# The last two token tiles of mLSTM's v and o share one pass over the weights

## The chip, the core and the metric

The kernel runs on one core of a Trainium2 chip. The time is device microseconds from the start to the end of one execution, lower is better. Three executions of the kernel before are given, and one more was recorded by the profiler; the trace of that one is what is read here.

## The reference, cut to what matters

One sequence of 512 tokens with 1024 features passes through two layers. The change touches one stage of the first layer, the mLSTM mixer: two of its four projections, `v` and `o`.

```python
def mlstm_mixer(h, w_in, i_bias, f_bias, conv_w, conv_b, norm_w, w_out):
    proj = h @ w_in
    qk = jax.nn.silu(causal_conv(proj[..., :2 * M_QK], conv_w, conv_b))
    q = split_heads(qk[..., :M_QK], M_HEADS)
    k = split_heads(qk[..., M_QK:], M_HEADS) * (M_DQK ** -0.5)
    v = split_heads(proj[..., 2 * M_QK:2 * M_QK + M_V], M_HEADS)
    o = proj[..., 2 * M_QK + M_V:2 * M_QK + 2 * M_V]
    ...
    hh = mlstm_chunkwise(q, k, v, i_pre, f_pre)
    hh = merge_heads(head_rmsnorm(hh, norm_w)) * jax.nn.sigmoid(o)
    return hh @ w_out
```

Every sub-layer is also modulated by (shift, scale, gate) = silu(c) @ ada_w + ada_b. That product is done on VectorE, in 80 small portions that are strewn through the stages (`ar`).

## The kernel before, in words

**Weights.** All dense weights lie in one list in the order in which they are used. A slot is 128x1024 values. Two slots come with one DMA into a tile `raw` (2 buffers, issued by SyncE). ScalarE copies a slot into a rounded tile `whi`, VectorE makes the rest `wlo` = raw - whi; both have 5 buffers (L400). A product is three matmuls: hi*hi, hi*lo, lo*hi. `Weights.get` (L234) returns a piece of a slot; it lets a slot go when its last user has passed and issues the ScalarE copies of slots for which a buffer is free (`want`). The VectorE subtractions of these are kept in a list and issued (`low`, L205) when `get` first reaches a new slot; with a subtraction the next load of `raw` is issued.

**The stage.** `main()` in `mlstm` computes the last two tiles of q and k, then v in two halves of 512 columns (a = 0, 1), then o in two halves. A half has four slots and four token tiles (`v00` to `v03`, `v10` to `v13`, `o00` and so on: half, tile). `tile_tok` computes one token tile: 24 matmuls over the four slots of the half. The first three tiles leave the slots where they are; the fourth lets each go when it has passed over it. So the slots of the next half find buffers only in the fourth tile, except the first of them, which has the fifth buffer. In this stage the slots 9 to 12 are v's first half, 13 to 16 the second, 17 to 20 and 21 to 24 those of o; `wlo14` is the second slot of v's second half, `wlo22` that of o's second half.

**After a tile.** A tile of v is copied to SBUF by ScalarE (`va`), then `ada()` issues one portion of the modulation on VectorE (`ar`, 128x1024, read from DRAM into 2 buffers; the load into a buffer is issued behind the portion that read it). A tile of o is copied by VectorE (`og`), then `ada(2)` issues two portions. After the four tiles of a half of o ScalarE applies the sigmoid.

**What sets the order around it.** `weave` (L336) runs `main()` and, at each `yield` of it, steps of side work as long as a plan of the engines' times says that VectorE and ScalarE are less than 3 us behind TensorE; two side jobs are open at a time. The side jobs are the gates, the convolutions (`conv`: ScalarE writes `qk`, VectorE adds three taps to it from the accumulator, later a silu; f = 0 to 7, `qk0` to `qk7`), the four head pairs (`pair`: scores `S`, decay `dt`, transposed keys `kp` and `kt`, states `cu` and `st`, outputs `nu`), and `close` (products `y`, transposes `tph`). All accumulators, those of side work too, come from one pool of 8 PSUM banks (L396); a tile takes a bank that an earlier one has left, and its first matmul waits until that one has been read. What `weave` and `Weights` decide is fixed when the program is built; on the chip each engine runs its own list in order.

After o, `out_proj` computes `m_out`; its first heads are closed by `y` on VectorE and `tph` on TensorE.

Of the kernel before, what the change touches and what calls it, by code (L numbers as in the profile page):

```python
# [10 lines left out]
F32 = mybir.dt.float32  # L11
# [4 lines left out]
AF = mybir.ActivationFunctionType  # L16
# [5 lines left out]
P = 128  # L22
D = 1024
T = 512
KT = D // P
NC = T // P
# [18 lines left out]
def _plan():  # L45
    plan, at = [], {}

    def add(name, blocks):
        at[name] = len(plan)
        plan.extend(blocks)  # L50

    k8 = range(KT)
    add("m_g0", [("m_qk", k, f) for k in k8 for f in (8, 0, 4, 1, 5, 2, 6)])
    add("m_qk", [("m_qk", k, f) for f in (3, 7) for k in k8])
    add("m_v", [("m_v", k, 4 * a + j) for a in range(2) for k in k8 for j in range(4)])
    add("m_o", [("m_o", k, 4 * a + j) for a in range(2) for k in k8 for j in range(4)])
    out_order = [(k, f) for k in k8 for f in range(4)] + [(k, f) for k in range(4) for f in range(4, 8)] + \
        [(k, f) for f in range(4, 8) for k in range(4, 8)]
    add("m_out", [("m_w_out", k, f) for k, f in out_order])
    for s in range(2):  # L60
        f0 = s * ET
        b = [("ffn", k, f) for k in k8 for f in (f0, FT + f0, f0 + 1, FT + f0 + 1)] if s == 0 else []
        for f in range(f0 + (2 if s == 0 else 0), f0 + ET):
            b += [("ffn", k, x) for x in (f, FT + f) for k in k8]
        add(f"f_in{s}", b)
        add(f"f_down{s}", [("ffn_w_down", f0 + f, d) for d in k8 for f in range(ET)])
    add("h_first", [("h_w_in", k, f) for k in k8 for f in (0, 8, 1, 9)])
    for what in H_ORDER:
        if what[0] == "h":
            h = int(what[1])  # L70
            add(what, [("h_w_in", k, f) for f in (h, 8 + h, h + 1, 9 + h) for k in k8])
        elif what[0] == "g":
            add("h_" + what, [("h_w_in", k, 24 + int(what[1]) + f) for f in range(4) for k in k8])
        else:
            add("h_" + what, [("h_w_in", k, 16 + 4 * int(what[1]) + j) for k in k8 for j in range(4)])
    add("h_out", [("h_w_out", k, f) for k, f in out_order])
    at["moe"] = len(plan)
    return plan, at


PLAN, AT = _plan()
# [306 lines left out]
class Kernel:  # L388
# [264 lines left out]
            if k % 2:  # L653
                yield

    def tile_tok(self, b, i, acc):

        mm = self.nc.tensor.matmul
        ts = slice(i * P, (i + 1) * P)
        for k in range(KT):  # L660
            hi, lo = self.W.get(b + 4 * k, 4, i == NC - 1)
            xh, xl = self.hn[k][0][:, ts], self.hn[k][1][:, ts]
            mm(acc, xh, hi, start=k == 0, stop=False)
            mm(acc, xh, lo, start=False, stop=False)
            mm(acc, xl, hi, start=False, stop=k == KT - 1)
            if k % 2:
                yield

    def out_proj(self, name, hh, l, side=lambda: None):

# [47 lines left out]
    def mlstm(self):  # L718
        nc, tc = self.nc, self.tc
        V, S = nc.vector, nc.scalar  # L720
        ident = self.C("ident")
        with ExitStack() as ctx:
# [5 lines left out]
            with tc.tile_pool(name="adf", bufs=6) as adf, tc.tile_pool(name="rawf", bufs=2) as rawf:  # L728
# [6 lines left out]
                accs = self.group_first("m_g0", 7, self.norm(0, 0, (a0,)))  # L735
            self.dump("hn0", [x for h in self.hn for x in h])
            self.big = ctx.enter_context(tc.tile_pool(name="big0", bufs=24))
            va_p = ctx.enter_context(tc.tile_pool(name="va", bufs=8))
# [28 lines left out]
            va, ys, og, hh, rsd, rows = {}, {}, {}, {}, {}, []  # L767
# [47 lines left out]
            def main():  # L815
                for n, f in enumerate((3, 7)):
                    acc = self.ps(f"qk{f}")
                    yield from self.tile_ws(AT["m_qk"] + 8 * n, self.hn, acc)
                    todo.append((f, acc))
                    self.ada()  # L820
                for a in range(2):
                    for i in range(NC):
                        acc = self.ps(f"v{a}{i}")
                        yield from self.tile_tok(AT["m_v"] + 32 * a, i, acc)
                        t = va_p.tile([P, 4, P + 1], F32, name=f"va{a}{i}", tag="va")
                        S.activation(t[:, :, 0:P], acc.rearrange("p (h d) -> p h d", h=4), AF.Copy)
                        nc.gpsimd.memset(t[:, :, P:P + 1], 1.0)
                        va[a, i] = t
                        self.ada()
                for a in range(2):  # L830
                    for i in range(NC):
                        acc = self.ps(f"o{a}{i}")
                        yield from self.tile_tok(AT["m_o"] + 32 * a, i, acc)
                        t = og[a, i] = self.slot(f"og{a}{i}")
                        V.tensor_copy(t, acc)
                        self.ada(2)
                    for i in range(NC):
                        S.activation(og[a, i], og[a, i], AF.Sigmoid)

# [110 lines left out]
            sides += [(lambda h=h: (h // 4, NC - 1) in og and h in rsd, close(h)) for h in range(4)]  # L950
            self.W.ahead = 4
            weave(nc.plan, main(), sides, 2, 0.0, 3.0)
            self.W.ahead = 3
            self.dump("y", [ys[a, c] for a in range(2) for c in range(NC)])
# [61 lines left out]
    def hgrn(self):  # L1016
        nc, tc = self.nc, self.tc
        V, S = nc.vector, nc.scalar
        ident = self.C("ident")
        with ExitStack() as ctx:  # L1020
# [19 lines left out]
            QK, LF, Q1, v, g, hh = {}, {}, {}, {}, {}, {}  # L1040
# [32 lines left out]
            def proj():  # L1073
                accs = self.group_first("h_first", 4, self.norm(1, 0))
                self.dump("hn1", [x for h in self.hn for x in h])
                for k in range(KT):
                    nc.gpsimd.dma_start(self.X[k], self.x[k])
                z = self.nrm.tile([P, T], F32, name="zero", tag="tmp")
                nc.gpsimd.memset(z, 0.0)
                for j in range(2):  # L1080
                    for i in range(0, NSLOT, P):
                        n = min(P, NSLOT - i)
                        nc.gpsimd.dma_start(self.XG[j][i:i + n], z[:n])
                evac(0, (accs[:2], accs[2:]))
                self.router()
                yield
                for what in H_ORDER:
                    w, n = what[0], int(what[1])
                    ps = []
                    for i in range(4):  # L1090
                        acc = self.ps(f"h{what}{i}")
                        if w == "h":
                            yield from self.tile_ws(AT[what] + 8 * i, self.hn, acc)
                            ps.append(acc)
                            if i == 3:
                                while not done >= {n - 3, n - 4}:
                                    yield "wait"
                                evac(n, (ps[:2], ps[2:]))
                            continue
                        t = new(f"{what}{i}", "vg", 12)  # L1100
                        if w == "v":
                            yield from self.tile_tok(AT["h_" + what], i, acc)
                            S.activation(t, acc, AF.Copy)
                            v[n, i] = t
                        else:
                            yield from self.tile_ws(AT["h_" + what] + 8 * i, self.hn, acc)
                            S.activation(t, acc, AF.Copy)
                            g[n + i] = t
                            if i >= 2:
                                gated(range(n + (i - 2) * 3, n + i + 1))  # L1110

            def gated(hs):

                for h in hs:
                    S.activation(g[h], g[h], AF.Silu)
                for h in hs:
                    if h in hh:
                        V.tensor_mul(hh[h], hh[h], g[h])
                    on.add(h)
# [146 lines left out]
            def main():  # L1266
                yield from proj()
                for _ in range(H - 2):
                    while next(out) == "wait":
                        yield "wait"  # L1270
                    yield
# [591 lines left out]
```

## Time and profile before

| | us |
|---|---|
| three executions | 1566.93, 1577.71, 1581.69 (median 1577.71) |
| the profiled execution | 1568.58 |
| its span, first to last instruction | 1566.8 |
| TensorE busy in it | 1490.4 (95%) |
| VectorE busy | 1087.0 (69%) |
| ScalarE busy | 845.4 (54%) |
| mean granted TensorE clock | 0.978 |

The stage of this change lies between about 76 and 216 us of the span. A row of the profile's waits says which engine waited for which, for how long in total, how often, and the longest. A row of the timeline gives start and duration (us), engine, line, operation, out<-in, shape, count, and in brackets the idle time of the engine before it and what ended it. Nearly all lines read L317, a helper through which every instruction is recorded, so rows are told apart by their tiles. The duration of a matmul is longer than its distance to the next, since matmuls are pipelined: 0.39 us stands for a distance of 0.23 us at the full clock, 0.63 for one of 0.43 at half of it.

### The profile page before, as it was taken

What the parts mean: (1) busy time and instruction counts of PE and PEld (TensorE: products, weight loads), DVE (VectorE), ACT (ScalarE), POOL (GpSimd) and SP (SyncE); (2) the same over time, 40 slices, a digit from 0 to 9 for tenths busy, and PEclk for the clock granted to TensorE, in tenths of its full rate; (3) what the DMA queues carried; (4) which work ended last, traced back from release to release, by engine and by line L of the source; (5) the groups of instructions that cost most, each with busy time, mean ns of one, the idle gap of its engine ahead of it and who ended that gap; (6) DMA issues with size and microseconds to landing.
All of it is one profiled execution on the core that took longest, in us unless ns stands there. A gap on an engine that the chain in (4) does not pass through costs nothing. (4 is left out here: it accounts for less than half of the span.)

```text
span 1566.8 us, 23572 instructions
## 1 busy us (share of the span) xinstructions
PE 1490.4 (95%) x8935; PEld 1310.8 (84%) x8935; DVE 1087.0 (69%) x1978; ACT 845.4 (54%) x1562; POOL 135.0 (9%) x213
## 2 busy tenths in 40 slices
PE   4989999999999999999999998999999999999995
PEld 3867776888888888688888875999999999999993
DVE  6886774655455545695977654687877878788795
ACT  5466333432222322365647543687786868777663
POOL 0041000000000000300000010501010010100142
PEclk9999999999999999999999999999999999999996
DMA  9462641445445553532102132788787887878782
GB/s 377 159 208 79 212 161 56 161 187 212 154 171 205 182 190 110 208 136 98 55 28 81 54 105 108 273 290 303 250 283 266 282 274 253 299 263 268 278 302 90
DMA packets 80854, 300.47 MB, mean 192 GB/s; under 512 B 8036, under 2 KB 8084, under 8 KB 79712
## 3 DMA queue, kind: packets, MB, share of 16 engines
q1 hardware_dynamic: 69424, 266.36, 47.9%
q0 software_dynamic: 11312, 32.56, 6.3%
q8 instruction: 72, 1.18, 0.3%
q14 instruction: 46, 0.38, 0.1%
HBM read 280.78 MB, written 18.09 MB: 191 GB/s over the span
## 5 line engine op out<-in xcount | busy, mean ns | idle before, releaser
L317 DVE TENSOR_TENSOR wlo<-raw,whi 128x1024 fp32r<-128x1024 f32 x403 | 489.6, 1222 | 106.4 <-ACT whi L317 104.3
L317 ACT ACTIVATE whi<-raw 128x1024 fp32r<-128x1024 f32 x403 | 422.0, 1055 | 182.0 <-DMA raw<-in_w 31.9
L317 PE MATMUL gu<-x,whi 128*128 128x304 f32 x1408 | 360.1, 345 | 2.1 <-DVE x L317 2.1
L317 PE MATMUL gu<-x,wlo 128*128 128x152 f32 x1408 | 328.5, 233 | 0.0
L317 PEld LDWEIGHTS gu<-x,wlo 128*128 128x128 f32 x1408 | 270.1, 192 | 0.0
L317 PEld LDWEIGHTS gu<-x,whi 128*128 128x128 f32 x1408 | 265.4, 189 | 2.5 <-DVE x L317 2.3
L317 PE MATMUL yd<-h,whi 128*128 128x304 f32 x704 | 181.6, 346 | 1.3 <-DVE h L317 1.3
L317 PE MATMUL yd<-h,wlo 128*128 128x152 f32 x704 | 163.8, 233 | 0.0
L317 PEld LDWEIGHTS yd<-h,wlo 128*128 128x128 f32 x704 | 134.5, 191 | 0.0
L317 PEld LDWEIGHTS yd<-h,whi 128*128 128x128 f32 x704 | 132.2, 188 | 1.6 <-DVE h L317 1.5
L317 DVE SCALAR_TENSOR_TENSOR ar<-ar,cond 128x1024 f32<-128x1024 f32 x80 | 98.4, 1232 | 3.9 <-DMA ar<-in_ada 3.8
L317 ACT ACTIVATE fhi<-fg 128x512 fp32r<-128x512 f32 x22 | 13.9, 633 | 114.3 <-DVE fg L317 114.3
L317 DVE TENSOR_TENSOR fg<-fg,fup 128x512 f32<-128x512 f32 x20 | 13.8, 688 | 82.7 <-PE fup L317 82.7
L317 PE MATMUL fd<-fhi,whi 128*128 128x512 f32 x176 | 69.6, 396 | 0.0
L317 PE MATMUL fd<-flo,whi 128*128 128x512 f32 x176 | 69.6, 396 | 0.0
L317 PE MATMUL fd<-fhi,wlo 128*128 128x512 f32 x176 | 69.6, 396 | 0.0
L317 ACT ACTIVATE t<-gu 128x152 f32<-128x152 f32 x176 | 47.9, 289 | 35.5 <-PE gu L317 33.5
L317 PE MATMUL fgp<-lo,whi 128*128 128x512 f32 x160 | 62.3, 389 | 0.0
L317 PE MATMUL fgp<-hi,whi 128*128 128x512 f32 x160 | 62.2, 389 | 0.0
L317 PE MATMUL fgp<-hi,wlo 128*128 128x512 f32 x160 | 62.2, 389 | 0.0
L317 PE MATMUL fup<-hi,whi 128*128 128x512 f32 x160 | 62.2, 389 | 0.0
L317 PE MATMUL fup<-lo,whi 128*128 128x512 f32 x160 | 62.2, 389 | 0.0
(404 smaller groups left out, 2988.5 us busy)
## 6 DMA issues: line engine op xcount, KB each, us to landing
raw<-in_moe SPq DMA_DIRECT2D x128, 1024.0 KB, 6.0
raw<-in_w SPq DMA_DIRECT2D x69, 1024.0 KB, 5.4
ar<-in_ada SPq DMA_DIRECT2D x80, 512.0 KB, 4.0
ad<-in_ada SPq DMA_DIRECT2D x8, 1024.0 KB, 14.8
XG<-zero POOLq DMA_DIRECT2D x18, 256.0 KB
xr<-XG POOLq DMA_DIRECT2D x28, 152.0 KB
raw<-in_moe SPq DMA_DIRECT2D x8, 512.0 KB, 3.5
Y<-yt POOLq DMA_DIRECT2D x14, 256.0 KB
```

The costliest lines, as they stand in the source:

```text
L317: r = f(*args, **kw)
```

## The change

`tile_tok` takes a list of tiles. The tiles 2 and 3 of every half of v and o go through the slots together: for each of the eight k, three matmuls for tile 2 and three for tile 3. Each slot is let go when both have passed over it, so the four go over 48 matmuls and not over 24. The copies of the two tiles and their portions of the modulation are issued after the shared pass, one tile behind the other. The shared pass yields to side work after every three matmuls, not six, and each copied tile is followed by one more yield. The second layer's use of `tile_tok` stays as it was (one tile in the list).

```diff
-    def tile_tok(self, b, i, acc):
+    def tile_tok(self, b, tiles, accs):
 
         mm = self.nc.tensor.matmul
-        ts = slice(i * P, (i + 1) * P)
         for k in range(KT):
-            hi, lo = self.W.get(b + 4 * k, 4, i == NC - 1)
-            xh, xl = self.hn[k][0][:, ts], self.hn[k][1][:, ts]
-            mm(acc, xh, hi, start=k == 0, stop=False)
-            mm(acc, xh, lo, start=False, stop=False)
-            mm(acc, xl, hi, start=False, stop=k == KT - 1)
-            if k % 2:
-                yield
+            hi, lo = self.W.get(b + 4 * k, 4, tiles[-1] == NC - 1)
+            for i, acc in zip(tiles, accs):
+                ts = slice(i * P, (i + 1) * P)
+                xh, xl = self.hn[k][0][:, ts], self.hn[k][1][:, ts]
+                mm(acc, xh, hi, start=k == 0, stop=False)
+                mm(acc, xh, lo, start=False, stop=False)
+                mm(acc, xl, hi, start=False, stop=k == KT - 1)
+                if k % 2 or len(tiles) > 1:
+                    yield
...
                 for a in range(2):
-                    for i in range(NC):
-                        acc = self.ps(f"v{a}{i}")
-                        yield from self.tile_tok(AT["m_v"] + 32 * a, i, acc)
-                        t = va_p.tile([P, 4, P + 1], F32, name=f"va{a}{i}", tag="va")
-                        S.activation(t[:, :, 0:P], acc.rearrange("p (h d) -> p h d", h=4), AF.Copy)
-                        nc.gpsimd.memset(t[:, :, P:P + 1], 1.0)
-                        va[a, i] = t
-                        self.ada()
+                    for tiles in ((0,), (1,), (2, 3)):
+                        accs = [self.ps(f"v{a}{i}") for i in tiles]
+                        yield from self.tile_tok(AT["m_v"] + 32 * a, tiles, accs)
+                        for i, acc in zip(tiles, accs):
+                            t = va_p.tile([P, 4, P + 1], F32, name=f"va{a}{i}", tag="va")
+                            S.activation(t[:, :, 0:P], acc.rearrange("p (h d) -> p h d", h=4), AF.Copy)
+                            nc.gpsimd.memset(t[:, :, P:P + 1], 1.0)
+                            va[a, i] = t
+                            self.ada()
+                            yield
                 for a in range(2):
...
+                        for i, acc in zip(tiles, accs):
+                            t = og[a, i] = self.slot(f"og{a}{i}")
+                            V.tensor_copy(t, acc)
+                            self.ada(2)
+                            yield
```

The program has as many TensorE instructions as before, 8467 rows of its list, and no VectorE or ScalarE instruction is added. The order changes at these places.

TensorE in v's first half, at the first scores `S0`, `S1` of head pair 0. Before, they stand near the end of tile v02, when v03 has no accumulator yet:

```order
L317 MATMUL v02_723<-whi11_520,lo4_364 128x512
L317 MATMUL v02_723<-whi11_520,hi5_393 128x512
L317 MATMUL v02_723<-wlo11_521,hi5_393 128x512
L317 MATMUL v02_723<-whi11_520,lo5_399 128x512
L317 MATMUL S0_748<-qk0_526,qk4_531 128x128
L317 MATMUL S1_749<-qk0_526,qk4_531 128x128
```

Now:

```order
L317 MATMUL v03_724<-whi9_457,lo1_256 128x512
L317 MATMUL v02_723<-whi10_516,hi2_286 128x512
L317 MATMUL v02_723<-wlo10_517,hi2_286 128x512
L317 MATMUL v02_723<-whi10_516,lo2_292 128x512
L317 MATMUL S0_749<-qk0_526,qk4_531 128x128
L317 MATMUL S1_750<-qk0_526,qk4_531 128x128
```

Both accumulators, v02 and v03, are open when the scores come, and 33 matmuls of the two tiles stand behind the scores, where 30 stood. The bank that v03 took from the convolution of `qk2` before (`m_g05`) is now the bank of `S1`.

VectorE at the turn from v's first half to its second, from the copy `dec0` of pair 0 to the first `wlo` that is needed. Before:

```order
L317 COPY dec0_806<-wb0_674 128x4
L317 TENSOR_TENSOR qk0_526<-qk0_526,wb0_674 128x512
L317 SCALAR_TENSOR_TENSOR qk3_818<-qk3_537,vec_93,qk3_818 128x511
L317 SCALAR_TENSOR_TENSOR qk3_818<-qk3_537,vec_93,qk3_818 128x510
L317 SCALAR_TENSOR_TENSOR qk3_818<-qk3_537,vec_93,qk3_818 128x509
L317 SCALAR_TENSOR_TENSOR ar4_721,mod0_119<-ar4_721,cond_91 128x1024
L317 TENSOR_TENSOR wlo14_787<-raw7_524,whi14_786 128x1024
```

Now:

```order
L317 COPY dec0_805<-wb0_667 128x4
L317 TENSOR_TENSOR qk0_526<-qk0_526,wb0_667 128x512
L317 SCALAR_TENSOR_TENSOR qk7_817<-qk7_570,vec_93,qk7_817 128x511
L317 SCALAR_TENSOR_TENSOR qk7_817<-qk7_570,vec_93,qk7_817 128x510
L317 SCALAR_TENSOR_TENSOR qk7_817<-qk7_570,vec_93,qk7_817 128x509
L317 SCALAR_TENSOR_TENSOR ar3_661,mod0_119<-ar3_661,cond_91 128x1024
L317 SCALAR_TENSOR_TENSOR ar4_721,mod0_119<-ar4_721,cond_91 128x1024
L317 TENSOR_TENSOR wlo14_743<-raw7_524,whi14_742 128x1024
```

The three taps of `qk3` now stand ahead of `dec0`; those of `qk7`, which stood behind the four `wlo`, have come ahead of them, and the portion `ar3`, which stood ahead of pair 0's two `dt`, now comes right ahead of `ar4`.

VectorE at the turn from o's first half to its second, from the copy of tile o03 (before) or o02 (now) to the first `wlo` that is needed. Before:

```order
L317 COPY og03_1545<-o03_1511 128x512
L317 SCALAR_TENSOR_TENSOR ar15_1506,mod0_119<-ar15_1506,cond_91 128x1024
L317 TENSOR_TENSOR mod0_119<-mod0_119,vec_93 128x8
L317 SCALAR_TENSOR_TENSOR ar16_1509,mod0_119<-ar16_1509,cond_91 128x1024
L317 TENSOR_TENSOR wlo22_1519<-raw11_1254,whi22_1518 128x1024
```

Now:

```order
L317 COPY og02_1537<-o02_1478 128x512
L317 SCALAR_TENSOR_TENSOR ar13_1473,mod0_119<-ar13_1473,cond_91 128x1024
L317 SCALAR_TENSOR_TENSOR ar14_1476,mod0_119<-ar14_1476,cond_91 128x1024
L317 COPY og03_1545<-o03_1479 128x512
L317 SCALAR_TENSOR_TENSOR ar15_1540,mod0_119<-ar15_1540,cond_91 128x1024
L317 TENSOR_TENSOR mod0_119<-mod0_119,vec_93 128x8
L317 SCALAR_TENSOR_TENSOR ar16_1543,mod0_119<-ar16_1543,cond_91 128x1024
L317 TENSOR_TENSOR wlo22_1493<-raw11_1376,whi22_1492 128x1024
```

`og02` and its two portions were done a tile earlier; now they stand behind the shared pass too, ahead of `og03`. At the end of o's second half the same eight rows stand ahead of the products `y` (`og12`, `ar21`, `ar22`, `og13`, `ar23`, two small sums, `ar24`, sixteen `y`).

## Rows read from the trace of the kernel before

**Rows 1.** Busy time, share of the span, instructions: part 1 of the page.

```profile
PE 1490.4 (95%) x8935; PEld 1310.8 (84%) x8935; DVE 1087.0 (69%) x1978; ACT 845.4 (54%) x1562; POOL 135.0 (9%) x213
```

**Rows 2.** Waits of TensorE, 60 to 300 us: total us, times, longest.

```profile
PE v L317 <- DVE wlo L317: 5.1, 1, 5.1
PE o L317 <- DVE wlo L317: 3.9, 1, 3.9
PE f_in L317 <- ACT hi L317: 3.0, 1, 3.0
PE nu L317 <- DVE dt L317: 2.4, 1, 2.4
PE tph L317 <- DVE y L317: 2.1, 2, 1.7
```

**Rows 3.** Timeline of TensorE at the turn to v's second half.

```profile
109.61 0.79 PE L317 MATMUL v<-wlo,hi 128*128 128x512 f32 x1 [5.14 <-DVE wlo L317]
```

**Rows 4.** Timeline of VectorE ahead of the same turn.

```profile
94.72 2.32 DVE L317 SCALAR_TENSOR_TENSOR qk<-m_g,vec,qk 128x511 f32<-128x511 f32 x3 [3.35 <-ACT qk L317]
...
102.18 1.57 DVE L317 COPY dec<-wb 128x4 f32<-128x4 f32 x1
103.41 0.68 DVE L317 TENSOR_TENSOR qk<-qk,wb 128x512 f32<-128x512 f32 x1
104.97 2.31 DVE L317 SCALAR_TENSOR_TENSOR qk<-qk,vec,qk 128x511 f32<-128x511 f32 x3 [0.88 <-ACT qk L317]
107.20 1.21 DVE L317 SCALAR_TENSOR_TENSOR ar<-ar,cond 128x1024 f32<-128x1024 f32 x1
...
108.34 4.62 DVE L317 TENSOR_TENSOR wlo<-raw,whi 128x1024 fp32r<-128x1024 f32 x4
```

**Rows 5.** Timeline of ScalarE ahead of the same turn.

```profile
98.84 1.06 ACT L317 ACTIVATE whi<-raw 128x1024 fp32r<-128x1024 f32 x1 [1.40 <-PE v L317]
...
101.22 1.15 ACT L317 ACTIVATE qk<-qk 128x512 f32<-128x512 f32 x2
...
104.17 0.76 ACT L317 ACTIVATE qk<-qk,vec 128x512 f32<-128x512 f32 x1
```

**Rows 6.** Timeline of TensorE at the scores of pair 0.

```profile
94.07 1.16 PE L317 MATMUL S<-qk,qk 64*128 64x128 f32 x14 [0.43 <-ACT va L317]
...
97.18 0.47 PE L317 MATMUL v<-whi,hi 128*128 128x512 f32 x1 [0.38 <-DVE qk L317]
```

**Rows 7.** Timeline of VectorE at the turn to o's second half.

```profile
179.65 1.23 DVE L317 SCALAR_TENSOR_TENSOR ar<-ar,cond 128x1024 f32<-128x1024 f32 x1 [1.05 <-DMA ar<-in_ada]
...
182.20 0.69 DVE L317 COPY og<-o 128x512 f32<-128x512 f32 x1 [1.32 <-PE o L317]
182.81 1.22 DVE L317 SCALAR_TENSOR_TENSOR ar<-ar,cond 128x1024 f32<-128x1024 f32 x1
...
185.19 1.23 DVE L317 SCALAR_TENSOR_TENSOR ar<-ar,cond 128x1024 f32<-128x1024 f32 x1 [0.95 <-DMA ar<-in_ada]
...
186.34 4.62 DVE L317 TENSOR_TENSOR wlo<-raw,whi 128x1024 fp32r<-128x1024 f32 x4
```

**Rows 8.** Timeline of VectorE at the end of o.

```profile
213.82 0.69 DVE L317 COPY og<-o 128x512 f32<-128x512 f32 x1 [1.72 <-PE o L317]
214.80 1.23 DVE L317 SCALAR_TENSOR_TENSOR ar<-ar,cond 128x1024 f32<-128x1024 f32 x1 [0.29 <-DMA ar<-in_ada]
...
216.64 1.22 DVE L317 SCALAR_TENSOR_TENSOR ar<-ar,cond 128x1024 f32<-128x1024 f32 x1 [0.21 <-DMA ar<-in_ada]
...
217.79 4.29 DVE L317 SCALAR_TENSOR_TENSOR y<-y,rsmy,og 128x128 f32<-128x128 f32 x16
```

**Rows 9.** Windows: length, busy us of the five engines, granted clock, DMA share, GB/s.

```profile
130.00:134.00 4.00, 1.22 (x7) 0.68 (x6) 3.66 (x15) 1.64 (x6) 1.39 (x4) 1.00 0.39 131
182.00:194.00 12.00, 8.14 (x24) 6.14 (x23) 9.88 (x18) 4.34 (x6) 0.00 (x0) 0.72 0.72 255
272.00:276.00 4.00, 4.00 (x13) 3.09 (x12) 2.47 (x4) 1.43 (x3) 0.00 (x0) 0.57 0.60 187
```

More of the change, by code (lines that the diff above doesn't have):

```diff
@@ L821, in main @@
                 for a in range(2):
-                    for i in range(NC):
-                        acc = self.ps(f"v{a}{i}")
-                        yield from self.tile_tok(AT["m_v"] + 32 * a, i, acc)
-                        t = va_p.tile([P, 4, P + 1], F32, name=f"va{a}{i}", tag="va")
-                        S.activation(t[:, :, 0:P], acc.rearrange("p (h d) -> p h d", h=4), AF.Copy)
-                        nc.gpsimd.memset(t[:, :, P:P + 1], 1.0)
-                        va[a, i] = t
-                        self.ada()
-                for a in range(2):
[L831 to L836, printed above, removed]
+                    for tiles in ((0,), (1,), (2, 3)):
[8 more added lines that the diff above has]
+                            yield
+                for a in range(2):
+                    for tiles in ((0,), (1,), (2, 3)):
+                        accs = [self.ps(f"o{a}{i}") for i in tiles]
+                        yield from self.tile_tok(AT["m_o"] + 32 * a, tiles, accs)
+                        for i, acc in zip(tiles, accs):
[3 more added lines that the diff above has]
+                            yield
                     for i in range(NC):
@@ L1101, in proj @@
                         if w == "v":
-                            yield from self.tile_tok(AT["h_" + what], i, acc)
+                            yield from self.tile_tok(AT["h_" + what], (i,), (acc,))
                             S.activation(t, acc, AF.Copy)
```

## The prediction

> **What bounds the kernel now.** I read the page first: TensorE is busy for 95% of the span [rows 1], so the change can gain only where TensorE stands still, and can lose wherever it makes TensorE stand still. The list of its waits shows where that is in this stage [rows 2]: 5.1 us in v and 3.9 us in o, both for a `wlo` of VectorE, and 2.1 us in `tph` for the products `y`. The reader is to see that two of these are the turns from the first half of v and of o to the second, and that neither names a `whi` of ScalarE. Then I followed the releaser back on its own engine. At v's turn VectorE runs three taps of a convolution at 104.97, a portion `ar` at 107.20 and the four `wlo` from 108.34, without a gap [rows 4]; TensorE goes on at 109.61 [rows 3]. ScalarE had begun the first of these `whi` at 98.84 [rows 5], long before the first `wlo`. So the `wlo` are late because of what stands ahead of them in VectorE's list. At o's turn it is the same: `og` at 182.20, `ar` at 182.81, a second `ar` that waits for its DMA until 185.19, then the `wlo` at 186.34 [rows 7]. At the end of o, `y` stands behind `og` at 213.82 and two `ar` [rows 8]. The question for the change is thus not when a slot is let go but what VectorE has to do between the last matmul of a half and the first `wlo`.
>
> **The change part by part.** The matmuls are the same in number and shape, so TensorE's own work costs nothing more. That slots are let go earlier brings the `whi` forward; they were not what TensorE waited for, and the `wlo` of a new half are still issued when `get` first reaches its slots, behind the two tiles' copies and portions. I take its gain as nothing; its bounds are nothing and the two waits.
>
> The first cost is at v's turn. Up to 92.8 us both orders bring the same work, so the times of before hold. `S1` now takes the bank of the convolution of `qk2`, which VectorE ends at 94.72 + 2.32 = 97.04 [rows 4]; before, `v03` waited for that bank until 97.18 [rows 6], after `S` and six matmuls of v02 had been done. Now `S` itself waits until 97.1. Its matmuls take some 1.1 us (1.16 for 14) [rows 6], so the shared pass goes on at 98.2. The second slot of the half is let go nine matmuls later: 98.2 + 8 x 0.23 + 0.39 = 100.4. ScalarE's `whi` of that slot's successor stands ahead of the silus and of the convolution's first step for `qk3`. Before, from the start of that `whi` to the end of the silus took 101.22 + 1.15 - 98.84 = 3.53, and the convolution's step 0.76 [rows 5]. So VectorE can start the taps of `qk3` at 100.4 + 3.5 + 0.8 = 104.7, about where it does now (104.97). From there it has to do the taps (2.23 until the next row), `dec0` and the product (some 0.8: 0.68 and a small copy), the taps of `qk7` (2.23), two portions (1.14 each) and the first `wlo`, after which TensorE started 1.27 behind its beginning [rows 3, 4]: 104.7 + 2.2 + 0.8 + 2.2 + 2.3 + 1.3 = 113.5. TensorE went on at 109.6, so this turn loses 3.9. Bounds: without the late `S` the taps of `qk3` would follow VectorE's own work at about 101.7, and the turn would lose 0.9; if `dec0` takes 1.57 again [rows 4] it loses 5.3. I take 3.9, because each link of that chain has a row.
>
> What stood behind the four `wlo` there, the taps of `qk7`, is done by then, so VectorE is free sooner afterwards; no wait of TensorE named in rows 2 hangs on that. The 2.4 us for `dt` stay: the reciprocal root of pair 0 and `dt` of pair 1 still follow one another on VectorE. The new run of `cu` and `nu` without tiles of o between them costs nothing that I can find: two pairs alternate there, and VectorE's small steps between are shorter than TensorE's.
>
> The second cost is at o's turn. Call C the moment at which the last tile's accumulator can be copied (182.20 before). TensorE went on at 186.34 + 1.27 = 187.61, C + 5.4 [rows 7]. Now `og02` is copied at C - 0.7 and `ar13` starts 0.6 later, at C - 0.1; `ar14` follows at C + 1.1 and `og03` at C + 2.2. The next portion uses the buffer that `ar13` has left. From the start of a portion to the start of the one that reads its buffer again takes 185.19 - 179.65 = 5.54 when VectorE waits for the load [rows 7]. So `ar15` starts at C + 5.5, `ar16` 1.15 and a small sum later at C + 6.8, and TensorE goes on 187.61 - 185.19 = 2.4 after that, at C + 9.2. This turn loses 3.8. If two loads in flight slow each other by some tenths it is 4.3; if they did not wait at all VectorE's own work alone would set C + 7.2, a loss of 1.8.
>
> The Trainium skill (DMA: Bandwidth & Descriptors, Anatomy of one DMA) gives a DMA a fixed 2.0 us and 436 GB/s, which for a portion of 512 KB is an estimate of 3.2 us, where the rows make it 5.54 - 1.23 = 4.3; by it this turn would lose 2.7 us, and the next one 1.1 less too. Its rule to issue a load early and wait late (Rules for kernel authors) speaks against the change here, since the shared pass issues two loads and waits for them at once.
>
> The third cost is at the end of o, by the same order. Now `y` starts at 217.79, C + 4.0 with C = 213.82 [rows 8]. After the change `ar23` starts at C + 5.5, `ar24` 1.6 later (216.64 - 214.80, less its wait of 0.21), `y` 1.15 after it, at C + 8.3 [rows 8]. It loses 4.3, between 2.3 and 4.8 by the same bounds. TensorE has only twelve matmuls of `m_out` there before `tph`.
>
> Sum: 3.9 + 3.8 + 4.3 = 12.0 us more. The clock is left out of the sum. The two waits for `wlo` are followed by the lower level: the granted clock is 0.72 over 182 to 194 [rows 9]. It falls there already, so the same price is paid before and after, unless the longer waits lengthen it.
>
> **The rivals.** First, the change does what it says and helps: if the `whi` had held the turns up, both waits would go, 5.1 + 3.9 = 9.0, and the half clock behind them, at most some 3 us each: 1568.6 - 15 = 1554. Rows 4, 5 and 7 speak against it. It decides in favour if the first `wlo` of a turn starts within 1.3 us of its `whi`.
>
> Second, the order changes but nothing is lost: the portions are covered, because VectorE comes to the turn with less behind it. Then the time stays within 4 us of 1568.6. VectorE does have gaps (an idle 3.35 us [rows 4]), but those lie ahead of the shared pass's end, and the copy `og02` cannot be done before it.
>
> Third, slower than the sum, by the clock. `S` now makes TensorE stand for about 3 us in a place where it stood for 0.4. A wait of 2.4 us (at 131 to 133) left the clock at full over 130 to 134 [rows 9]; a wait of 3.0 us in `f_in` was followed by a granted clock of 0.57 over 272 to 276 [rows 2, 9]. If it falls, the nine matmuls on which the chain of v's turn hangs take some 2 us more; at `tph`, a wait of about 6 us instead of some 2 would give back up to 3 us at the half level. Sum 12 + 5 = 17, 1585.6. The Trainium skill (TensorE: Matmul & The Clock Gate, HAM oscillation) says that a gap in which TensorE waits lowers its clock for what follows; by that rule this rival holds, and the rows of this trace agree for the longer waits but not for the one of 2.4 us.
>
> **How the numbers follow.** Against the profiled execution (1568.58, span 1566.8) the sum gives 1580.6. The runs shown lie from 1566.93 to 1581.69 around it, their median 9.1 above it; the sum on the median would be 1589.7. I take the middle, 1585. Forecast (8 to 16 us more): 0.58. Third rival (over 16): 0.22. Second rival (within 4 to 8): 0.13. First rival (a gain): 0.07. For the range I leave out the first rival and the far end of the third: 4 us more on the lowest base gives 1573, 18 more on the highest 1600. About 1% is what a measurement of this kernel can tell from no change, that is 15.7 us: the sum lies below it by 4, so most of the forecast counts as the same. Faster 0.06, same 0.64, slower 0.30.
>
> **What would show it.** In the profile of the changed kernel TensorE should wait for VectorE at four places: at `S` for `qk`, some 3 us; at v's second half for `wlo`, 6 to 7 us instead of 5.1; at o's second half for `wlo`, 7 to 8 us instead of 3.9; at `tph` for `y`, about 6 us instead of 2.1. In VectorE's timeline the two turns of o should show `og`, two `ar`, `og`, then two `ar` of which at least the first waits for DMA for some 2 us. The prediction is wrong if the `wlo` waits shrink, if the second pair of `ar` doesn't wait, or if TensorE's granted clock falls in new places.

## The result, and the profile after

| | before | after |
|---|---|---|
| median of 14 executions, us | 1575.53 (1565.74 to 1581.69) | 1589.5 (1584.37 to 1594.32) |
| ratio after / before, 95% interval | | 1.0083 (1.0064 to 1.0103) |
| the profiled execution, us | 1568.58 | 1592.53 |
| its span | 1566.8 | 1590.7 |
| mean granted clock | 0.978 | 0.968 |

The change makes the kernel 14.0 us slower by the medians; the ratio puts it at 0.83%. Its interval is clear of 1, and a difference of this size still counts as the same. The prediction said 12.0 us more, 1585 from 1573 to 1600.

The two profiled executions differ by 23.9 us, and not all of it is the change. The first matmul of the next stage (`f_in`) starts at 270.5 us before and at 284.1 after. The order behind this stage is the same in both programs. Most of the rest comes at the start of the expert stage (`gu`), over which the distance of the two profiles grows from 12.6 to 21.6 us (another 3 come at the very end). The profile after has waits of TensorE there that end on nothing that the profile shows:

```profile
PE gu L317 <- issue: 6.4, 4, 4.1
```

The windows of the first 10 us of that part, before and after (length, busy us of the five engines, granted clock, DMA share, GB/s), show that less was moved there and that the clock was lower:

```profile
988.00:998.00 10.00, 7.86 (x51) 7.68 (x50) 6.89 (x15) 5.85 (x10) 8.66 (x13) 0.83 0.62 216
```

```profile
1000.00:1010.00 10.00, 5.90 (x32) 5.72 (x32) 4.52 (x5) 3.24 (x6) 8.45 (x14) 0.72 0.48 165
```

From `f_in` to the end the profile of before took 1296.3 us, that of after 1306.6. In the experiments below it is 1301 to 1309 in those that ran together first (e1, e2, e4) and 1290 to 1298 in the others, beside which the kernel before ran faster too (medians of 1566 to 1567 and not 1577): it goes with the group in which they ran, each group on another chip, and not with their edits. So I read the stage by itself: from the copy of v's first tile (`va` of v00, 83.73 before, 82.97 after) to the first matmul of `f_in`. It takes 186.8 us before and 201.1 after: 14.3 more, which agrees with the medians.

TensorE's busy time is nearly the one of before [rows 1]; its waits in the stage are not [rows 2]:

```profile
PE 1496.0 (94%) x8935; PEld 1316.8 (83%) x8935; DVE 1087.4 (68%) x1978; ACT 846.9 (53%) x1562; POOL 133.0 (8%) x213
```

```profile
PE o L317 <- DVE wlo L317: 7.7, 1, 7.7
PE tph L317 <- DVE y L317: 6.6, 2, 6.3
PE v L317 <- DVE wlo L317: 5.7, 1, 5.7
PE nu L317 <- DVE dt L317: 3.7, 1, 3.7
PE f_in L317 <- ACT hi L317: 3.0, 1, 3.0
PE S L317 <- DVE qk L317: 2.6, 1, 2.6
```

All four waits that were named are there: `S`, v's turn, o's turn, `tph`. The one at v's turn is 5.7 us, a little under the 6 to 7 that were named. At the scores, where rows 6 had 0.43, the timeline of TensorE after shows this:

```profile
93.68 0.48 PE L317 MATMUL S<-qk,qk 64*128 64x128 f32 x2 [0.69 <-ACT va L317]
96.79 2.05 PE L317 MATMUL S<-qk,qk 64*128 64x128 f32 x14 [2.62 <-DVE qk L317]
98.76 0.79 PE L317 MATMUL v<-whi,hi 128*128 128x512 f32 x1
99.36 0.63 PE L317 MATMUL v<-wlo,hi 128*128 128x512 f32 x1
```

The matmuls take 0.63 us, so the clock is at half right behind this wait. ScalarE ahead of v's turn (compare rows 5):

```profile
103.01 1.06 ACT L317 ACTIVATE whi<-raw 128x1024 fp32r<-128x1024 f32 x1 [7.10 <-PE v L317]
...
105.38 1.16 ACT L317 ACTIVATE qk<-qk 128x512 f32<-128x512 f32 x2
106.44 0.76 ACT L317 ACTIVATE qk<-qk,vec 128x512 f32<-128x512 f32 x1
```

VectorE at the same turn (compare rows 4), and TensorE behind it (compare rows 3):

```profile
107.23 2.32 DVE L317 SCALAR_TENSOR_TENSOR qk<-qk,vec,qk 128x511 f32<-128x511 f32 x3 [6.51 <-ACT qk L317]
...
109.54 0.68 DVE L317 TENSOR_TENSOR qk<-qk,wb 128x512 f32<-128x512 f32 x1
110.14 2.31 DVE L317 SCALAR_TENSOR_TENSOR qk<-qk,vec,qk 128x511 f32<-128x511 f32 x3
112.36 1.22 DVE L317 SCALAR_TENSOR_TENSOR ar<-ar,cond 128x1024 f32<-128x1024 f32 x1
...
113.50 1.22 DVE L317 SCALAR_TENSOR_TENSOR ar<-ar,cond 128x1024 f32<-128x1024 f32 x1
...
114.65 4.63 DVE L317 TENSOR_TENSOR wlo<-raw,whi 128x1024 fp32r<-128x1024 f32 x4
```

```profile
115.93 0.80 PE L317 MATMUL v<-wlo,hi 128*128 128x512 f32 x1 [5.72 <-DVE wlo L317]
```

The chain is the predicted one, link by link, but some 2.5 us late from `whi` on (103.01, not 100.4). VectorE at o's turn (compare rows 7) and at the end of o (compare rows 8):

```profile
189.03 0.69 DVE L317 COPY og<-o 128x512 f32<-128x512 f32 x1 [3.49 <-PE o L317]
189.63 1.22 DVE L317 SCALAR_TENSOR_TENSOR ar<-ar,cond 128x1024 f32<-128x1024 f32 x1
...
191.92 0.69 DVE L317 COPY og<-o 128x512 f32<-128x512 f32 x1
194.43 1.22 DVE L317 SCALAR_TENSOR_TENSOR ar<-ar,cond 128x1024 f32<-128x1024 f32 x1 [1.83 <-DMA ar<-in_ada]
...
196.48 1.22 DVE L317 SCALAR_TENSOR_TENSOR ar<-ar,cond 128x1024 f32<-128x1024 f32 x1 [0.62 <-DMA ar<-in_ada]
```

```profile
223.15 0.69 DVE L317 COPY og<-o 128x512 f32<-128x512 f32 x1 [7.22 <-PE o L317]
...
226.04 0.69 DVE L317 COPY og<-o 128x512 f32<-128x512 f32 x1
228.53 1.23 DVE L317 SCALAR_TENSOR_TENSOR ar<-ar,cond 128x1024 f32<-128x1024 f32 x1 [1.81 <-DMA ar<-in_ada]
...
231.20 1.23 DVE L317 SCALAR_TENSOR_TENSOR ar<-ar,cond 128x1024 f32<-128x1024 f32 x1 [1.03 <-DMA ar<-in_ada]
...
232.35 4.28 DVE L317 SCALAR_TENSOR_TENSOR y<-y,rsmy,og 128x128 f32<-128x128 f32 x16
```

Both show `og`, two `ar`, `og`, then two `ar` that wait for their loads. TensorE at o's turn, before and after:

```profile
187.61 0.79 PE L317 MATMUL o<-wlo,hi 128*128 128x512 f32 x1 [3.86 <-DVE wlo L317]
```

```profile
198.91 0.79 PE L317 MATMUL o<-wlo,hi 128*128 128x512 f32 x1 [7.65 <-DVE wlo L317]
```

### The profile page after: what moved, and what is told of

The parts are those of the page before. It is cut to its first block, busy times and chain, and to the rows that moved or that the text cites. A ratio compares the mean times of both kernels' runs of the same rounds, so it can differ in the third digit from the quotient of the medians.

```text
span 1590.7 us, 23577 instructions
## 1 busy us (share of the span) xinstructions
PE 1496.0 (94%) x8935; PEld 1316.8 (83%) x8935; DVE 1087.4 (68%) x1978; ACT 846.9 (53%) x1562; POOL 133.0 (8%) x213
## 5 line engine op out<-in xcount | busy, mean ns | idle before, releaser
L317 PE MATMUL gu<-x,whi 128*128 128x304 f32 x1408 | 363.9, 347 | 4.1 <-issue 4.1
```

What stands on the lines that cost most here:

```text
L317: r = f(*args, **kw)
```

## The experiments

The theory: TensorE waits at a turn for what VectorE has queued ahead of the first `wlo` (or `y`), and the shared pass puts more there. The rivals: the loss of one turn is made up at the next; the shared pass itself costs, by its accumulators or the clock; the `whi` or the loads hold the turns up. The stage column is from the copy of v00 to the first matmul of `f_in`, in the profile of each kernel. The ratio is that of whole times to the kernel before, run on the same chip. Each stage comes from one profiled execution, and executions differ: after, e1 and e10 have the same order on TensorE, VectorE and ScalarE up to v's turn and reach it 33.0, 29.2 and 31.7 us after the copy of v00. So a difference of under 4 us between two stages can be chance.

| kernel | edit | stage, us | ratio, 95% interval |
|---|---|---|---|
| before | | 186.8 | |
| after | | 201.1 | 1.0083 (1.0064 to 1.0103) |
| e1 | only v shared | 194.0 | 1.0021 (0.9989 to 1.0052) |
| e2 | only o shared | 193.8 | 1.0031 (1.0011 to 1.0050) |
| e3 | after, portions within the passes | 187.9 | not read |
| e4 | before, portions within the tiles | 177.5 | 0.9931 (0.9913 to 0.9949) |
| e5 | after, early `wlo` | 191.6 | 1.0036 (1.0025 to 1.0047) |
| e6 | before, early `wlo` | 182.7 | 0.9967 (0.9953 to 0.9981) |
| e10 | after, three buffers for portions | 195.4 | 1.0054 (1.0036 to 1.0073) |
| e11 | before, three buffers | 183.4 | 0.9974 (0.9961 to 0.9987) |
| e9 | e3 with three buffers, `y` put right | 182.5 | 0.9985 (0.9975 to 0.9995) |
| e8 | before, e4 and e6 together | 174.4 | 0.9955 (0.9938 to 0.9972) |
| e12 | e8 with three buffers | 172.4 | 0.9921 (0.9904 to 0.9938) |
| e7 | after with all three edits | 176.1 | 0.9933 (0.9916 to 0.9949) |

**One half of the change alone.** In e1 the loop over o's tiles is put back (the extra yield too), in e2 that of v.

```diff
-                    for tiles in ((0,), (1,), (2, 3)):
+                    for tiles in ((0,), (1,), (2,), (3,)):
```

> Only v's last two tiles share a pass; o is as before. Theory (each turn costs by what VectorE has queued ahead of the first wlo or y, and the turns add up): v's turn as in the changed kernel, TensorE goes on at 115.9 us (109.6 before) after a wait of some 5.7 us for wlo, S stands 2.6 us; o's turn as before, wait 3.9 us for wlo; tph waits some 2 us. The next stage's first matmul (f_in, 270.5 before, 284.1 in the changed kernel) starts at 277 to 278, and the time is 6 to 8 us more than before. Rival (v's loss is made up again in o, because TensorE is then no longer ahead of VectorE): f_in at 271 to 273, and the time within 2 us of before.

> Only o's last two tiles share a pass; v is as before. Theory: v's turn as before (109.6, wait 5.1 us), o's turn waits 7.7 us for wlo instead of 3.9, tph some 6.3 us for y instead of 2.1; f_in starts at 277.5 to 279, and the time is 7 to 9 us more than before. With v alone the two losses add up to the 14 us of the whole change. Rival (the loss at o hangs on v's: portions and pairs that v pushed into o's first half): waits of o and tph within 1.5 us of before, f_in at 270 to 273.

Counted from the copy of v00, TensorE passes these points at:

| | v's turn | o's turn | `tph` | `f_in` |
|---|---|---|---|---|
| before | 25.9 | 103.9 | 134.6 | 186.8 |
| after | 33.0 | 115.9 | 149.9 | 201.1 |
| e1, v alone | 29.2 | 111.8 | 141.7 | 194.0 |
| e2, o alone | 25.5 | 107.5 | 142.0 | 193.8 |

Each half loses 7 us by the stage, and nothing is made up: the first rival falls. The whole times are too coarse to show it: the ratio is 1.0021 for e1, with 1 in its interval, and 1.0031 for e2. e2 does what was expected, with waits of 8.2 and 6.2 us. e1 holds the best test of v's chain: it has after's order up to there and the same wait at `S`, but its clock stayed up. The windows of after and of e1:

```profile
98.00:106.00 8.00, 8.00 (x30) 6.31 (x28) 2.69 (x4) 2.96 (x4) 2.77 (x3) 0.67 0.19 64
```

```profile
98.00:106.00 8.00, 8.00 (x37) 6.50 (x36) 4.13 (x7) 5.44 (x7) 3.99 (x6) 1.00 0.36 100
```

And the chain of e1 on TensorE, ScalarE and VectorE:

```profile
97.08 1.13 PE L317 MATMUL S<-qk,qk 64*128 64x128 f32 x14 [2.62 <-DVE qk L317]
...
113.46 0.80 PE L317 MATMUL v<-wlo,hi 128*128 128x512 f32 x1 [5.93 <-DVE wlo L317]
```

```profile
100.53 1.07 ACT L317 ACTIVATE whi<-raw 128x1024 fp32r<-128x1024 f32 x1 [4.34 <-PE v L317]
```

```profile
104.77 2.32 DVE L317 SCALAR_TENSOR_TENSOR qk<-qk,vec,qk 128x511 f32<-128x511 f32 x3 [3.76 <-ACT qk L317]
```

Predicted were 98.2, 100.4, 104.7 and 113.5. v's turn loses 3.4 here (29.2 against 25.9), 7.1 in after. Of these 3.7 us, 2.8 lie behind `S`: from where `S` goes on to the turn it is 16.4 us in e1 at the full clock, as predicted, and 19.1 in after. The other 1.0 lies ahead of `S`, where one portion (`ar`, at 85.33 in after) took 2.27 us in after and 1.29 in e1. That e1 loses 4.6 us more on the way to o's turn was not expected, so its total, which came out as expected, did so in part by luck. Two rows of its profile answer for part of it: `nu` waits 3.7 us (2.4 before), and o's turn 6.1 instead of 3.9, since six of the eight portions of o's first half now wait for their loads (three before), 0.8 to 1.9 us each.

**The portions moved out of the turn.** `tile_tok` gets a list of k after which it issues a portion; the calls behind the copies go. e3 from after (shared pass (1, 5) for v and (0, 2, 4, 6) for o), e4 from before ((3,) and (1, 5)).

```diff
+            if k in at:
+                self.ada()
...
-                            self.ada(2)
```

> The changed kernel, with the modulation's portions issued within the passes (v: in a single tile after k = 3, in the shared pass after k = 1 and 5; o: after k = 1 and 5, in the shared pass after k = 0, 2, 4, 6) and not behind the copies. Theory (the copies and portions queued behind the shared pass are the loss): o's turn has og, eight products y (2.15 us, which come ahead of wlo in this order) and then wlo, so the wait falls from 7.7 to about 3.5 to 4.5 us; at tph two og stand ahead of y and the wait falls from 6.3 to 0 to 2 us; v's turn loses the two portions and the taps of qk7 ahead of wlo, wait 5.7 to about 1 to 3 us. f_in starts at 268 to 274 instead of 284.1, and the time is within 5 us of the kernel before. Rival (the shared pass itself costs, by its accumulators held together or its slots let go late): waits of 6 us or more stay at two of the three places, f_in at 280 or later.

> The kernel before (four single tiles), with the portions issued within the tiles (v after k = 3, o after k = 1 and 5) and not behind the copies. Theory (what VectorE has ahead of wlo and y at a turn sets TensorE's wait, whatever the order of the tiles): o's turn has og alone ahead of wlo, TensorE goes on about 2.0 us after the accumulator is done instead of 5.4, so its wait falls from 3.9 to 0 to 1 us; tph waits 0 to 1 us instead of 2.1; v's turn waits 1 to 2 us instead of 5.1. f_in starts at 259 to 263 instead of 270.5 and the time is 7 to 12 us less than before. Rival (the portions only move their own cost and their loads: a portion that waits for its DMA within a tile makes the convolutions and pairs late, and so TensorE): f_in at 269 to 275, time within 4 us of before.

e4 is the plain case: no tile is shared, only the portions stand elsewhere. The waits for `wlo` go from 5.1 and 3.9 us to these, and the stage is 9.3 us shorter:

```profile
PE v L317 <- DVE wlo L317: 3.9, 1, 3.9
...
PE o L317 <- DVE wlo L317: 0.5, 1, 0.5
```

At v's turn I had expected 1 to 2: three taps, two `dt`, one portion and `dec0` still stand there, one behind the other from 99.44 to the first `wlo` at 105.74. e3's stage is where it was expected, but not by the expected way: v's wait is 4.1 (expected 1 to 3), and o's grew to 8.5 (expected 3.5 to 4.5). Its VectorE ahead of o's turn:

```profile
177.54 1.23 DVE L317 SCALAR_TENSOR_TENSOR ar<-ar,cond 128x1024 f32<-128x1024 f32 x1 [3.76 <-DMA ar<-in_ada]
...
182.37 1.23 DVE L317 SCALAR_TENSOR_TENSOR ar<-ar,cond 128x1024 f32<-128x1024 f32 x1 [1.86 <-DMA ar<-in_ada]
...
184.96 1.23 DVE L317 SCALAR_TENSOR_TENSOR ar<-ar,cond 128x1024 f32<-128x1024 f32 x1 [1.35 <-DMA ar<-in_ada]
...
187.45 1.23 DVE L317 SCALAR_TENSOR_TENSOR ar<-ar,cond 128x1024 f32<-128x1024 f32 x1 [1.06 <-DMA ar<-in_ada]
...
188.60 1.28 DVE L317 COPY og<-o 128x512 f32<-128x512 f32 x2
```

With two buffers the loads come every 2.5 us or more, and the copies `og` stand behind the last. (In e3 `y` also takes o before its sigmoid: the yield behind the last copy lets `close` run ahead of it, and eight `y` stand ahead of the `wlo`. In the changed kernel they come behind the four `wlo`. What follows in e3 leaves that sigmoid out, so its time as a whole, 4209 us, is not read.)

**More room for the loads.** Three buffers instead of two, and one less for the stage's tiles.

```diff
-        self.ada_room = [self.adp] * 2
+        self.ada_room = [self.adp] * 3
...
-            self.big = ctx.enter_context(tc.tile_pool(name="big0", bufs=24))
+            self.big = ctx.enter_context(tc.tile_pool(name="big0", bufs=23))
```

> The changed kernel with three buffers for the portions of the modulation instead of two, and 23 instead of 24 in the pool of the stage's tiles to make room for it; VectorE's order at the turns is the same. Theory (of the two turns of o, VectorE's own work is 7.2 us and the rest is the wait for a portion's load): the waits for DMA of 1.8 and 0.6 us at o's turn and of 1.8 and 1.0 at the end of o go; o's wait falls from 7.7 to 5.3 to 5.9 us, tph's from 6.3 to 3.4 to 4.2. f_in at 278 to 280.5 instead of 284.1. Rival (the loads are limited by what the DMA engines move, so a third in flight lengthens each): the waits for DMA stay at 2 us or more at each place, f_in at 283 to 285.

> The kernel before with three buffers for the portions and 23 for the stage's tiles. Theory: the wait for DMA of 0.95 us ahead of o's turn and of 0.2 to 0.3 at the end of o go, and VectorE comes to the turn with the earlier portions done; o's wait falls from 3.9 to 2.5 to 3.2 us, tph's from 2.1 to 1.5 to 2; f_in at 268.5 to 270 instead of 270.5, time within 3 us of before. So the portions' loads cost the kernel before little and the changed one 4 to 5 us. Rival: as with the changed kernel, no change; or a wait for a tile of the smaller pool makes it slower (f_in at 272 or later).

> The changed kernel with the portions within the passes and three buffers for them (23 for the stage's tiles), and without the yield behind the last tile of a half of o, so that the products y come behind wlo and take o after its sigmoid (in the run with two buffers, e3, they stood ahead of both, so y took o before its sigmoid, and what follows m_out in that run is not read). There o's wait was 8.5 us and not 3.5 to 4.5, since the portions in the shared pass waited 3.8, 1.9, 1.4 and 1.1 us for their loads and the copies og stood behind them. Theory (loads): with three buffers these waits shrink to less than 2.5 us in sum, o's wait falls to 0.3 to 3 us, the stage from 187.9 to 179 to 184 us (v00's copy to f_in). Rival (the shared pass itself makes the portions late, since og00 and og01 come later in it): o's wait 6 us or more.

In e10 the waits for loads at o's turn are down to one of 0.37 us, with the same order:

```profile
192.12 1.22 DVE L317 SCALAR_TENSOR_TENSOR ar<-ar,cond 128x1024 f32<-128x1024 f32 x1
...
193.92 1.23 DVE L317 SCALAR_TENSOR_TENSOR ar<-ar,cond 128x1024 f32<-128x1024 f32 x1 [0.37 <-DMA ar<-in_ada]
```

o's wait is 5.5, `tph`'s 3.7, the stage 5.7 us shorter than after's. e11 gains 3.4, a little more than expected, with waits of 2.8 and 1.0. In e9 two waits for loads stay, 2.72 and 0.77 us (under 2.5 in sum were expected), and o's wait falls from 8.5 to 2.0. Two things differ from e3 there: VectorE's waits for loads are 4.5 us shorter in sum, and the eight `y`, about 2.1 us, no longer stand ahead of the `wlo`. So most of e3's miss was the loads. A third load in flight shortened these waits, in e9 and e10.

**The subtraction earlier.** In `get`, what `want` has left is issued when the next slot is let go.

```diff
+        if self.used is not None:
+            self.low(self.left)
+            self.left = []
         self.free()
```

> The changed kernel, with the subtraction wlo of a slot issued when the next slot is let go, and not when the new half first needs it; the portions stay behind the copies. Now wlo14, wlo15 and wlo22, wlo23 stand ahead of the turn, wlo16 and wlo24 behind the same copies and portions as before. Theory (the queue ahead of the wlo that is needed): TensorE runs two slots further, 12 matmuls or 2.8 us, and then waits for wlo24: o's wait 7.7 falls to about 5; v's 5.7 to 1 to 3; tph's 6.3 for y stays, since y stands behind the same work. f_in starts at 275 to 279 instead of 284.1, the time is 5 to 9 us less than the changed kernel's. Rival (whi or the load of raw comes too late, so an earlier wlo makes VectorE stand): VectorE waits 1 us or more for whi ahead of these wlo, and f_in stays at 282 or later.

> The kernel before, with the subtraction wlo of a slot issued when the next slot is let go. Theory: v's wait falls from 5.1 to about 2.4 us and o's from 3.9 to about 1, tph's some 2 us stays; the half clock behind the two waits shortens by 1 to 3 us. f_in at 262 to 266 instead of 270.5; time 4 to 8 us less than before. If letting the slots go over twice the time is worth something, it is here that it must show: then the changed kernel with the same edit lies nearer to the kernel before with it than 10 us (f_in); if it is worth nothing the two keep the distance of 13.6 us less the 1 to 3 us that the two slots of start bring more to the longer waits. Rival (VectorE stands for whi): f_in at 269 or later.

e5 came as expected: v's wait 2.1, o's 5.6, `tph`'s 5.6. VectorE stood once for a `whi`, 1.49 us, and still the stage lost 9.5 us. So `whi` did not hold the turns in the changed kernel: the same `whi`, with the `wlo` issued earlier, left shorter waits. e6 gained 4.1, less than expected: v waits 4.5 in two pieces, o 2.3, and `nu` 3.6 instead of 2.4. These gains of e6 and e11 are small beside what chance does to a stage, but both ratios lie clear below 1. The distance of the two kernels is 8.9 us, under the 10 that I had set as a sign that the sharing is worth something; but e6 lost some of its own at `nu`, so this pair doesn't decide it.

**All of it.** e8 has the portions within the tiles and the early `wlo`, e12 three buffers too, e7 the same as e12 with the shared passes (and no yield behind the last tile of a half of o).

> The kernel before, with both edits: portions issued within the tiles, and the subtraction wlo of a slot issued when the next slot is let go. Counted from the copy of the first tile of v (v00) to the first matmul of f_in, the stage took 186.8 us in the kernel before, 201.1 in the changed one, 177.6 with the portions within the tiles alone and 182.7 with the early wlo alone. Theory (both remove the same thing, work queued ahead of a wlo): the two gains don't add, v's wait of 3.9 us that the portions' edit left goes to 0 to 1.5, its half clock with it; o's stays under 1; 172 to 176 us for the stage, and a time 10 to 15 us less than before. Rival (the two edits only trade places in VectorE's list): 177 or more.

> The same kernel with three buffers for the portions and 23 in the pool of the stage's tiles. Theory: with the queue ahead of the wlo gone, a portion that waits for its load hardly matters; 0 to 2 us less than with two buffers, stage 171 to 176 us, time 10 to 16 us less than before. Rival (VectorE's waits for the loads still set o's speed): 4 us less or more.

> The changed kernel with all three edits (portions within the passes, early wlo, three buffers with 23 tiles, no yield behind the last tile of a half of o). Against the kernel before with the same three edits (sent beside it) it tells what sharing the pass is worth when VectorE's queue at the turns is out of the way. Theory (sharing itself neither helps nor harms but for S, which still stands some 1.5 to 2.6 us, and the half clock that may follow): stage 1 to 6 us longer than that kernel's, time the same or up to 7 us more. Rival (slots let go over twice the time help once nothing else is in the way): stage 2 us shorter or more. Second rival (sharing itself costs, whatever is queued): stage 9 us longer or more, as between the two kernels with the early wlo alone (8.9) or the portions alone (10.3).

Stages of 174.4, 172.4 and 176.1 us, all as the theory had them. The time of e8 fell by 8.8 us by the medians, where 10 to 15 were expected. The time of e12 fell by more against e8 than its stage did, 4.3 us by the medians, as its rival had it, against 2.0; in the profiles the rest lies behind the stage (1294.9 us from `f_in` to the end in e8, 1290.2 in e12), and I did not trace it further. e12's waits in the stage, beside `f_in`:

```profile
PE nu L320 <- DVE dt L320: 2.7, 1, 2.7
PE v L320 <- DVE wlo L320: 2.2, 2, 1.3
PE tph L320 <- DVE y L320: 0.8, 2, 0.6
```

And e7's:

```profile
PE nu L320 <- DVE dt L320: 5.1, 1, 5.1
...
PE S L320 <- DVE qk L320: 1.6, 1, 1.6
PE tph L320 <- DVE y L320: 0.8, 2, 0.6
```

In e7 no turn waits for a `wlo` any more, in v or in o, where e12 still waits 2.2 us in v. That doesn't show that the slots let go over twice the time bring something: e7 reaches the first matmul that needs `wlo14` 24.7 us after the copy of v00, e12 21.0, so VectorE had more time. e7 pays 1.6 us at `S`, which e12 doesn't, and 2.4 us more at `nu`, and the granted clock over the 8 us behind these two waits is 0.79 each time (1.00 in e12 behind `nu`). In all its stage is 3.7 us longer, which can be chance; the whole times differ by 2.9 us by the medians, and the intervals of the two ratios overlap. So sharing shows no gain even here, and what it costs with the queue cleared stays open. e12 is the fastest kernel, 0.8% below the one before.

The change also yields to side work more often, in the shared pass and behind each copy. No run tries these yields apart from the sharing, so how much of the new order comes from either is not shown.

## Why the prediction was right, and where it was off

- **What bounds the turns: right.** The `wlo` stand behind other work of VectorE. Taking the portions away (e4, e9) or issuing the `wlo` earlier (e5, e6) shortens the waits; the change, which lets the slots go over twice the time, makes them longer. The first rival falls.
- **v's turn: the mechanism right, the size off.** The term was 3.9 and came out as 7.1. The step that failed is "The clock is left out of the sum". With the clock at full the chain gave 3.4 (e1). The lower clock behind `S` put 2.8 on it: 1.9 on the nine matmuls, which the third rival had priced at 2, and 0.9 on those of `S`, which had no price. The other 1.0 is the later `S`. The first part of that rival came true in this execution, not in e1. By one of the signs that the prediction named itself, a granted clock that falls in new places, it was wrong here.
- **"The 2.4 us for dt stay": wrong.** `nu` waits 3.7 us in after, where 2.4 left the clock at full before [rows 9]. From v's turn to o's turn the loss grew by 5.0 us, of which 3.8 are the term of o; the 1.2 left is about what this wait grew by, though nothing ties the two more closely. Behind it the granted clock is 0.71 over 135 to 139.
- **o's turn: right.** C is 191.92 - 2.2 = 189.7, and TensorE went on at 198.91, C + 9.2 as predicted. The way there differs a little: the first load was back after 194.43 - 189.63 - 1.23 = 3.6 us and not 4.3, the second after 196.48 - 190.78 - 1.23 = 4.5, and the second decided. The 3.2 us estimated from the Trainium skill (DMA: Bandwidth & Descriptors, Anatomy of one DMA) come near the first, but by them alone the turn would have lost 2.7; the page's figures were fitted to DMAs that GpSimd issues, and these loads are issued by SyncE.
- **The end of o: right in the chain, smaller in effect.** `y` starts at 232.35, C + 8.5 (predicted C + 8.3). From o's turn to `tph` the loss is 34.0 - 30.7 = 3.3 and not 4.3, because the matmuls between o's turn and the end of o went faster: granted clock 0.93 over 198.9 to 223.8, 0.88 before over 187.6 to 213.8. The length of the wait does not explain that: in e2 a longer one, 8.2 us, was followed by 0.89 over the same matmuls, and the loss is 3.8. So the smaller effect is luck of this execution, as far as the runs show. Behind `tph` the third rival expected up to 3 us more at half the clock; it took 1.0 less, with 0.97 before and after.
- **The sum.** 7.1 + 1.2 + 3.8 + 3.3 is 15.4; 1.0 comes back between `tph` and `f_in` (51.2 us against 52.2), which I did not trace. That is, but for rounding, the 14.3 of the stage, where 12.0 was predicted. The misses have both signs and cancelled in part, which is luck.
- **The base.** The sum on the median (1589.7) was nearer to the result (1589.5) than the middle that I took. That it hit is luck too: the median of three was 2.2 us above that of 14, and the sum 2.3 under the stage's loss. The profiled execution lies near the fast end of its kernel, so a stage's loss should have been put on the median.

## What to carry to other kernels

Before letting buffers go earlier, look which of the two operations that refill them ends last, and what stands ahead of it on its own engine; here it was the second one, and the work that the loop puts behind a tile. Joining two tiles also joins what follows them: two copies and four portions came at once at the one point where TensorE could not go on without VectorE. Moving such filler into the loop, issuing the subtraction as each slot is let go, and one more buffer for the filler's loads took 14 us off the stage without any sharing.

## What I had not expected of the hardware

A wait of the same length at the same place was followed by either level of the clock. TensorE stood 2.6 us at `S` in after, e1, e5 and e10, with the same order of its matmuls up to there; over the 8 us from where it went on, the granted clock was 0.60 in after, 0.79 in e10, and 1.00 in e1 and e5. What came just before was not quite the same: in after and e10 TensorE had also stood 0.7 us ahead of the first matmuls of `S`, in e1 and e5 it had not. But in e3, e7 and e9 a wait of only 1.6 to 1.7 us was followed by 0.79 too. At `nu`, waits of 2.6 to 2.8 us were followed by 0.79 in e9 and e10 and by 1.00 in e3, e8 and e12. The Trainium skill (TensorE: Matmul & The Clock Gate, HAM oscillation) ties a lower clock to the gaps in which TensorE waits, when they are long enough; here a gap of one length was followed by it in some executions and not in others, and its price was 2.8 us in after against e1.
